# A two-layer encoder on one core: queries and splits moved a block ahead in attention, two PSUM banks kept across its borders, and four reorderings of sums and splits further on

## The chip, the cores and the metric

The kernel runs on one core of a Trainium2 chip. The metric is the device time of one execution in microseconds (us); before the change it is 1671.56, the median of three runs (1671.12 to 1671.75).

## What is computed

The reference is a trunk of two layers with shared weights over two requests, a prompt of 512 tokens and a sample of 256, D = 1024, all float32. The kernel treats both as one matrix of T = 768 tokens, kept transposed (features on partitions).

```python
for i in range(2):
    h = rms_norm(x, norm_mix[i])
    if i == 0:   # 16 heads of 64, 4 key/value groups, keys within 128 tokens, T5 bias, a sink logit per head
        x = x + window_attention(h, attn_w_qkv[0], attn_w_o[0], attn_sink[0], band_bias, in_window)
    else:        # (b_gate * conv3(c_gate * u)) @ w_out
        x = x + short_conv(h, conv_w_in[0], conv_w[0], conv_w_out[0])
    h = rms_norm(x, norm_mlp[i])
    x = x + jnp.square(jax.nn.relu(h @ mlp_w_up[i])) @ mlp_w_down[i]      # hidden size 4096
    gate = jax.nn.sigmoid(rms_norm(x, norm_ple[i]) @ ple_w_gate[i])
    x = x + (p[i] @ ple_w_proj[i]) * gate
return rms_norm(x, final_norm)
```

In attention a block of 128 queries meets the two or three key blocks around it; the softmax has the sink logit in its maximum and its sum.

## The kernel before

**Arithmetic.** A float32 product is made of three matmuls of a rounded type: every operand is split in a high part (a copy on ScalarE, ACT) and a low part (source minus high part, on VectorE, DVE), and high x high, high x low and low x high are added up in PSUM. Tile names carry it: whi and wlo, zhi and zlo, vhi and vlo are parts of a weight, xs those of an activation, aos those of an attention output. Weights come as raw tiles (wraw) by DMA from SyncE (SP). Some low parts are made without DVE: `added` (L453, L455) writes the negative high part on ACT and lets an accumulating DMA, issued by GpSimd (POOL), add the weight onto it.

**Stages.** First `mixer_attention`: norm, keys, values and queries of the first heads, then `attend(g)` for the four key/value groups, each over six query blocks n (four of the prompt, two of the sample). A block (g, n) makes for each of four heads a score tile S on TensorE (PE) (L716, L717), adds the bias and takes the maximum on DVE (L718), the exponential on ACT (L738), scales by the reciprocal sum (one head on ACT, L744, three on DVE, L746), transposes (pt, L751), splits the transposed weights in ph (ACT, L759) and pl (DVE, L760), and multiplies by the values (O, L761, L762). Then come the output projection (`first_head`, `first_tail`: L129), the MLP, the gated embedding (`ple`), the convolution mixer, its projection, the second MLP and the second gated embedding.

**Work beside attention.** The order of instructions in the attention stage is set by a scheduler from the dependences and the order in the code. Its PE would run dry while a block's softmax is under way, so the table `beside` puts other work behind certain blocks: `queries(c)` (the queries of two heads: product, split in qh and ql, and the DMAs of L633 that lay them out as q), `keys1`, `projected` (a projection of the per-layer embedding, whose results go out as pjs), `begin_output` (splits the heads of the first two groups into aos) and `first_output` (the first part of the output projection, whose sums go to xa, L785). Queries stand behind blocks (g, 2) and (g, 4), the projection behind (1, 5), the output's two steps behind (2, 5).

**PSUM.** There are eight banks. The attention stage uses one pool with S and product tiles until keys, values (vp, evicted to vv at L667) and first queries are done, then another (scores S 3 banks, products 2, O 1, pt 2); after attention all eight are in a third pool with the tags A, C and B (4, 2 and 2 banks). A new pool's tile waits for the release of the old pool's tiles in whose banks it lies. `fresh` hands out the tags in the cycle A, C, A, B; `shift` counts them.

**After attention** the order of PE, ACT and DVE is that of the code. The MLP and the convolution work on chunks of weights (`Weights7`): two raw tiles give seven products instead of eight, from four parts (w11 and w12, "direct"; w21 and w22, "second") and sums of them, s3 and s2 ("s32", made by `sums32`, L417 and L418, and split in zhi and zlo) and s1 and s4 ("s14", `sums14`, L422 and L423). `high`, `low` and `split` make the parts of such a group (L442 on ACT, L462 on DVE). `up_begun` and `up_first` begin the first MLP while the norm is still being computed; its plain chunk (L1183) uses "direct" through the tiles zhi and zlo and "second" through whi and wlo. `up_plain` follows, and then `up` for the remaining chunks, with the first of them treated apart (`first`). Each chunk prepares the next chunk's weights v between its own products; `late()` issues the activations that the previous chunk left over. Matmuls of one product carry tile names a, b, c and d (L484). In the convolution mixer `plain` (L1759) does the first chunk and `seven` the others.

Of the kernel before, what the change touches and what calls it, by code (L numbers as in the profile page):

```python
# [11 lines left out]
F32 = mybir.dt.float32  # L12
# [3 lines left out]
PSUM = bass.MemoryType.PSUM  # L16
DRAM = bass.MemoryType.DRAM

P = 128
D = 1024  # L20
KB = D // P
# [8 lines left out]

BM, BS, BO, BT, BL = 1, 3, 1, 2, 5

# [15 lines left out]
def trunk_kernel(ctx: ExitStack, tc: tile.TileContext, a: dict, out: bass.AP):  # L48
# [7 lines left out]
    stat = ctx.enter_context(tc.tile_pool(name="stat", bufs=1))  # L56
    dram = ctx.enter_context(tc.tile_pool(name="dram", bufs=1, space=DRAM))

    act.preload_act_table_set(EXP_LN)
    tmp, turn, shift = None, 0, 0  # L60

# [43 lines left out]
    def bank(tag, name):  # L105
        return psum.tile([P, 512], F32, tag=tag, name=name, bufs=BANKS[tag])

# [381 lines left out]
    def mixer_attention():  # L489
# [10 lines left out]
        def pair(j, name, dt=F32):  # L500
            return main.tile([P, 2, T], dt, tag=f"x{j}", name=name)
# [40 lines left out]
        with tc.manual_schedule(engines=order):  # L542
# [39 lines left out]

            bp = psum.tile([P, 512], F32, tag="S", name="bp", bufs=2)
            pe.matmul(bp[:HEADS, :], lhsT=rb[:], rhs=oh[:], start=True, stop=True)
# [6 lines left out]
        with s1:  # L591
# [46 lines left out]
            rc = ap.tile([P, T // P], F32, name="rc", bufs=1)  # L638
            rt = psum.tile([P, 512], F32, tag="S", name="rt", bufs=2)
            for n in range(T // P):  # L640
# [15 lines left out]
            def values(n):  # L656
                ps = psum.tile([P, 512], F32, tag="S", name="vp", bufs=2)
                for k in range(KB):
                    xh, xl = (xs[i][k][:, n * P : (n + 1) * P] for i in range(2))
                    wh, wl = wv[0][k], wv[1][k]  # L660
                    pe.matmul(ps[:, :256], lhsT=xh, rhs=wh, start=k == 0, stop=False)
                    pe.matmul(ps[:, :256], lhsT=xh, rhs=wl, start=False, stop=False)
                    pe.matmul(ps[:, :256], lhsT=xl, rhs=wh, start=False, stop=k == KB - 1)
                src = ps[:, :256].rearrange("p (g d) -> p g d", g=KV)
                hi, lo = vv[:, n, :, 0, :], vv[:, n, :, 1, :]
                act.activation(hi, src, AF.Copy, scale=rc[:, n : n + 1])
                dve.scalar_tensor_tensor(lo, src, rc[:, n : n + 1], hi.bitcast(F32), ALU.mult, ALU.subtract)  # L667
# [25 lines left out]
            bands(0)  # L693

            def attend(g):
                heads[g] = pair(g, "heads")
                if g < KV - 1:
# [3 lines left out]
                for s in SEQS:  # L701
                    hi_blk = lo_blk + s // P
                    for n in range(lo_blk, hi_blk):
# [6 lines left out]
                        for hp in range(2):  # L710
                            L = ap.tile([P, 2, 384], F32, tag="L", name="L", bufs=BL)
                            for j in range(2):
                                h = REP * g + 2 * hp + j
                                S = psum.tile([P, 512], F32, tag="S", name="S", bufs=BS)
                                q = qst[h][:, n * P : (n + 1) * P]
# [91 lines left out]

            def projected():
                w = weight(a["proj"][1, 0], 2)
                for m in range(KB // 2):  # L810
                    step(1, m, w, part1, "t", False)

# [10 lines left out]
            def begin_output():  # L823
# [166 lines left out]
    def first_tail(norm, places, output, product, ws):  # L990
# [10 lines left out]
        c = ws[1]  # L1001
        m6, m7 = KB - 1, KB // 2 - 1
        ps = [output(m) for m in (m6, m7)]
        pjs.extend(product(m) for m in range(KB // 2))
        add(m6, ps[0], xa[m6])
# [23 lines left out]
    def mlp(l, norm, nxt, w, places, early, product=None, begun=None):  # L1029
# [5 lines left out]
        groups = [{k: {} for k in QS7.values()} for _ in range(NG)]  # L1035
        pend = []

# [77 lines left out]
        def up_first(ps, w, v, parts, s1):  # L1115
# [30 lines left out]
            for i in range(2):  # L1146
                for o in range(2):
                    rectified(y[i], ps[i][o], H * o, H * o + H, ALU.max)
                if i == 0:
# [5 lines left out]
                    s3.high(1)  # L1155
                    s3.added(1)
            pend.extend(acts_of(0, *y, y[1]))
            return v

        def up_plain(u, w, make, then):  # L1160
# [15 lines left out]
            for n, (i, ks, sides) in enumerate(order):  # L1176
# [15 lines left out]
                elif begun and n == 1:  # L1192
# [3 lines left out]
                    steps[1]()  # L1196
                    steps[2]()
                    v.split("direct")
                    steps[3]()
# [50 lines left out]
        def up(u, w, make, then):  # L1250
# [181 lines left out]
    def ple(norm, nxt):  # L1432
# [38 lines left out]
        with tc.manual_schedule(engines={ET.Activation, ET.PE, ET.DVE}):  # L1471
# [187 lines left out]
    def mixer_conv(norm, w, v, norm_parts, held, finals, places, nxt):  # L1659
# [124 lines left out]
        def seven(kind, p, w, make, first, last):  # L1784
# [186 lines left out]
```

## Time and profile before

| | us |
|---|---|
| median of three runs | 1671.56 |
| profiled execution | 1671.81 |
| its span | 1669.8 |
| PE busy in it | 1641.9 |
| DVE busy | 1381.3 |
| ACT busy | 949.1 |
| POOL busy | 71.9 |

The profile is of one execution; all times inside it count from the start of its span, and its own time is 2.0 longer than the span. An idle time in brackets is what an engine stood still ahead of an instruction, with the instruction that let it go. L12 is line 12 of the kernel before. The matmuls' ends are modelled, so a matmul shows as busy a little past the start of the next one.

### The profile page before, as it was taken

The page shows a single profiled execution, that of the slowest core. Times are in us where ns is not written, and L with a number is a line of the kernel's source. Part 1 is how long each engine was busy: PE and PEld are TensorE (multiplying, and loading weights), DVE is VectorE, ACT ScalarE, POOL GpSimd, SP SyncE. Part 2 cuts the span into 40 slices and gives each one's busy share as a digit, 9 for nine tenths or more (in the row PEclk, how much of TensorE's full clock was granted, in tenths as well). Part 3 has the DMA queues.
Part 4 walks back from the last instruction along what each step waited for, and adds up shares of the span by engine and source line. Part 5 has one row for each costly group of instructions (what it writes and reads, how often), then busy time and mean ns, then how long its engine had stood idle before and what let it go on. Part 6 is the DMA issues. An engine that isn't in the chain of part 4 may idle for free.

```text
span 1669.8 us, 24311 instructions
## 1 busy us (share of the span) xinstructions
PE 1641.9 (98%) x9414; PEld 1588.0 (95%) x9414; DVE 1381.3 (83%) x2242; ACT 949.1 (57%) x1508; POOL 71.9 (4%) x104
## 2 busy tenths in 40 slices
PE   8999999999999999999999999999999999999997
PEld 7888788999999999999999999999999999999986
DVE  7499888789889889877888787868889988988676
ACT  7377756765555556554654334545556555655454
POOL 0211000010000000000000000000000000000000
PEclk9999999999999999999999999999999999999998
DMA  8755312433333322341312222122333223333132
GB/s 265 192 152 144 101 59 75 121 96 82 95 95 95 94 85 77 93 123 64 101 61 76 76 66 76 61 76 64 95 95 95 87 78 90 95 95 106 65 92 98
DMA packets 55476, 161.11 MB, mean 96 GB/s; under 512 B 7056, under 2 KB 10128, under 8 KB 55360
## 3 DMA queue, kind: packets, MB, share of 16 engines
q1 hardware_dynamic: 45184, 139.89, 26.2%
q0 software_dynamic: 10176, 19.67, 6.7%
q8 instruction: 74, 1.21, 0.3%
q14 instruction: 42, 0.34, 0.1%
HBM read 138.82 MB, written 10.48 MB: 89 GB/s over the span
## 4 chain that ended last, share of the span: by engine, by line
PE 84%; DVE 9%; ACT 4%; issue 2%; DMA 1%; SPq 0%; DVEq 0%; ACTq 0%
PE a L484 31%; PE mm L129 10%; PE mm L138 8%; PE b L484 8%; PE c L484 4%; PE d L484 4%; PE B L484 4%; PE C L484 4%; PE gate L138 3%; PE pt L751 1%; PE p L1080 1%; PE p L1183 1%; PE gate L129 1%; PE O L761 1%; PE S L716 1%
## 5 line engine op out<-in xcount | busy, mean ns | idle before, releaser
L484 PE MATMUL a<-xs,whi 128*128 128x384 f32 x624 | 121.7, 336 | 0.0
L442 ACT ACTIVATE vhi<-wraw 128x512 fp32r<-128x512 f32 x67 | 42.2, 630 | 132.3 <-PE B L484 87.9
L484 PEld LDWEIGHTS a<-xs,whi 128*128 128x128 f32 x624 | 110.1, 188 | 0.1
L484 PE MATMUL a<-t,zhi 128*128 128x384 f32 x536 | 109.1, 336 | 0.0
L484 PE MATMUL a<-t,whi 128*128 128x384 f32 x536 | 108.8, 336 | 0.0
L484 PE MATMUL b<-t,zhi 128*128 128x384 f32 x536 | 108.7, 336 | 0.0
L1329 DVE TENSOR_TENSOR x<-x,a 128x384 f32<-128x384 f32 x112 | 62.1, 554 | 55.2 <-PE a L484 55.2
L484 PE MATMUL a<-act,whi 128*128 128x384 f32 x448 | 96.6, 337 | 0.0
L484 PEld LDWEIGHTS a<-t,whi 128*128 128x128 f32 x536 | 94.9, 188 | 0.0
L484 PEld LDWEIGHTS b<-t,zhi 128*128 128x128 f32 x536 | 94.9, 188 | 0.0
L484 PEld LDWEIGHTS a<-t,zhi 128*128 128x128 f32 x536 | 94.8, 188 | 0.0
L462 DVE TENSOR_TENSOR wlo<-wraw,whi 128x1024 fp32r<-128x1024 f32 x70 | 85.3, 1219 | 7.6 <-ACT whi L442 7.6
L442 ACT ACTIVATE whi<-sum 128x1024 fp32r<-128x1024 f32 x67 | 70.6, 1054 | 27.1 <-PE a L484 22.7
L462 DVE TENSOR_TENSOR wlo<-sum,whi 128x1024 fp32r<-128x1024 f32 x67 | 81.8, 1221 | 5.0 <-ACT whi L442 5.0
L1042 ACT ACTIVATE y<-y 128x768 f32<-128x768 f32 x64 | 53.7, 839 | 56.0 <-DVE y L1039 55.9
L138 PE MATMUL mm<-xs_mix,whi 128*128 128x512 f32 (+1 forms) x320 | 83.1, 342 | 0.0
L462 DVE TENSOR_TENSOR zlo<-sum,zhi 128x1024 fp32r<-128x1024 f32 x67 | 81.6, 1217 | 0.0
L484 PEld LDWEIGHTS a<-act,whi 128*128 128x128 f32 x448 | 79.8, 188 | 0.0
L442 ACT ACTIVATE whi<-wraw 128x1024 fp32r<-128x1024 f32 x72 | 75.7, 1051 | 6.8 <-PE C L484 6.8
L442 ACT ACTIVATE zhi<-sum 128x1024 fp32r<-128x1024 f32 x67 | 70.9, 1058 | 10.8 <-DVE sum L418 9.9
L484 PE MATMUL a<-xs,wlo 128*128 128x384 f32 x312 | 67.1, 336 | 0.0
L83 ACT ACTIVATE whi<-wraw 128x1024 fp32r<-128x1024 f32 (+2 forms) x49 | 49.9, 1019 | 29.5 <-PE mm L129 9.7
(345 smaller groups left out, 4555.4 us busy)
## 6 DMA issues: line engine op xcount, KB each, us to landing
wraw<-in_up SPq DMA_DIRECT2D x64, 512.0 KB, 3.7
wraw<-in_down SPq DMA_DIRECT2D x64, 512.0 KB, 4.2
wraw<-in_w_in SPq DMA_DIRECT2D x24, 512.0 KB, 3.5
wraw<-in_gate SPq DMA_DIRECT2D x16, 512.0 KB, 3.5
vlo<-in_up POOLq DMA_DIRECT2D x28, 256.0 KB, 5.5
vlo<-in_down POOLq DMA_DIRECT2D x28, 256.0 KB, 5.8
pj<-pjs SPq DMA_DIRECT2D x16, 384.0 KB, 2.9
wraw<-in_w_q SPq DMA_DIRECT2D x8, 512.0 KB, 4.6
```

The source lines that it names most:

```text
L83: first = act.activation(hi, src, AF.Copy)
L129: pe.matmul(t, lhsT=w, rhs=x[:, o:e], start=first and i == 0 and j == 0, stop=last and i == n - 1 and j == 2)
L138: pe.matmul(ps[:, o:e], lhsT=w, rhs=x[:, o:e], start=i == 0 and j == 0, stop=i == n - 1 and j == 2,)
L442: act.activation(hi[:], src, AF.Copy)
L462: dve.tensor_tensor(lo[:], src, hi[:].bitcast(F32), ALU.subtract)
L484: pe.matmul(ps, lhsT=a, rhs=b, start=start and i == 0, stop=i == len(terms) - 1, skip_group_check=True)
L716: pe.matmul(S[:, :w], lhsT=q, rhs=khh[g][:, k0 * P : k0 * P + w], start=True, stop=False)
L751: pe.transpose(pt[:, h * P : (h + 1) * P], lg[h // 2][:, h % 2, b * P : (b + 1) * P], ident[:],)
L761: pe.matmul(O[:], lhsT=v, rhs=ph[:], start=b == 0, stop=False)
L1042: act.activation(t[:], t[:], AF.Square)
L1080: pe.matmul(ps[o], lhsT=wt[:, c], rhs=xs[f"x{h + 1}{1 + o}"][m][part], start=k == 0 and j == 0, stop=k == KB - 1 and j == 2,)
L1329: dve.tensor_tensor(t[:, o : o + H], t[:, o : o + H], f, op)
```

## The change

No product is added or left out. Six things are moved.

1. A pool `pair_of_banks` with two PSUM banks lives for the whole kernel, and tag B always comes from it; the small products bp and rt, the values' product vp and two of three score tiles S use it too. The third score tile has one bank of the stage's pool. `shift` begins at 2 and is lowered by two in `first_tail`, so that the first output product lies in B and the tags further on stay mostly as they were.
2. In attention, queries go behind blocks (g, 1) and (g, 3), the projection is halved over (1, 4) and (1, 5), and `begin_output` goes behind (2, 4).
3. In the first MLP's beginning, the "direct" weight is split ahead of the "second" one and of the activations' low parts, and one `added` of an activation moves into the next chunk.
4. In both MLPs the first `up` chunk gets the order of the others.
5. At the border to the convolution, `sums32` moves behind the residual's last block.
6. In three of the convolution's chunks the low part of "s32" is made ahead of the product's last step `top`.

```diff
+    pair_of_banks = ctx.enter_context(tc.tile_pool(name="psB", bufs=2, space=PSUM))
-    tmp, turn, shift = None, 0, 0
+    tmp, turn, shift = None, 0, 2
...
     def bank(tag, name):
-        return psum.tile([P, 512], F32, tag=tag, name=name, bufs=BANKS[tag])
+        pool = pair_of_banks if tag == "B" else psum
+        return pool.tile([P, 512], F32, tag=tag, name=name, bufs=BANKS[tag])
...
-                ps = psum.tile([P, 512], F32, tag="S", name="vp", bufs=2)
+                ps = bank("B", "vp")
...
+            def third():
+                return psum.tile([P, 512], F32, tag="S", name="S", bufs=1)
...
-                                S = psum.tile([P, 512], F32, tag="S", name="S", bufs=BS)
+                                S = third() if scores % 3 == 1 else bank("B", "S")
+                                scores += 1
...
             beside = {
                 (0, 5): (inputs1, keys1),
-                (1, 5): (projected,),
-                (2, 5): (begin_output, first_output),
+                (1, 4): (lambda: projected(0),),
+                (1, 5): (lambda: projected(1),),
+                (2, 4): (begin_output,),
+                (2, 5): (first_output,),
             }
...
-                    beside[g, 2 + 2 * n] = (lambda c=2 * g + 2 + n: queries(c),)
+                    beside[g, 1 + 2 * n] = (lambda c=2 * g + 2 + n: queries(c),)
...
         ps = [output(m) for m in (m6, m7)]
+        shift -= 2
...
-            v.added("second")
+            v.high("direct")
             s1.low(0)
             s1.low(1)
-            v.high("direct")
             s2.t13()
             s2.high(0)
             v.low("direct")
+            v.added("second")
...
                     s3.high(1)
-                    s3.added(1)
             pend.extend(acts_of(0, *y, y[1]))
+            aside.append(lambda: s3.added(1))
...
             if seven:
-                if not first:
-                    v.sums14()
+                v.sums14()
                 v.high("s32")
-            if not first:
-                late()
+            late()
...
-            if first:
-                late()
-                if seven:
-                    v.sums14()
             late()
...
-            v.sums32()
             added()
             nxt.plain_block(m, x(m))
+            v.sums32()
...
             product7(a, w, "s4", xs, False)
+            if busy and not last:
+                v.low("s32")
             top(kind, p, a, H)
```

On DVE at the entry to `attend`, around the last value tile's eviction (vv) and the first scores' reductions (L718, which is L727 after), before:

```order
L84 TENSOR_TENSOR ql<-qt,qh 128x768
L667 SCALAR_TENSOR_TENSOR vv<-vp,rc,vv 128x4x64
L718 ISA L,mx<-S,bias,sink 128x256
L718 ISA mx 128x1
L718 ISA L,mx<-S,bias,sink 128x256
```

The same place after:

```order
L85 TENSOR_TENSOR ql<-qt,qh 128x768
L727 ISA L,mx<-S,bias,sink 128x256
L727 ISA mx 128x1
L669 SCALAR_TENSOR_TENSOR vv<-vp,rc,vv 128x4x64
L727 ISA L,mx<-S,bias,sink 128x256
```

The first score's reduction has passed the last eviction.

On DVE where the head tiles are split (aos), between block (2, 5)'s reductions and its scales, before (nm, es and sm are a block's maxima and sums):

```order
L718 ISA L,mx<-S,bias,sink 128x256
L718 ISA mx 128x1
L84 TENSOR_TENSOR aos<-heads,aos 128x768
L769 TENSOR_TENSOR heads<-O,ot 64x2x128 x2
L731 TENSOR_SCALAR nm<-mx 128x4
L733 TENSOR_TENSOR es<-sink,mx 128x4
L84 TENSOR_TENSOR aos<-heads,aos 128x768 x3
L739 TENSOR_TENSOR sm<-sm,es 128x4
```

After, a block earlier, the first split stands among the scales of a block (L755), and further down three stand together:

```order
L749 RECIPROCAL sm<-sm 128x4
L85 TENSOR_TENSOR aos<-heads,aos 128x768
L755 TENSOR_SCALAR L<-L,sm 128x256
L769 TENSOR_TENSOR pl<-pt,ph 128x512
L755 TENSOR_SCALAR L<-L,sm 128x256 x2
```

```order
L778 TENSOR_TENSOR heads<-O,ot 64x2x128 x2
L740 TENSOR_SCALAR nm<-mx 128x4
L742 TENSOR_TENSOR es<-sink,mx 128x4
L85 TENSOR_TENSOR aos<-heads,aos 128x768 x3
L748 TENSOR_TENSOR sm<-sm,es 128x4
```

One split has moved ahead; the three others still stand in a row ahead of the next block's sums.

On ACT at the beginning of the first MLP (q and t are steps of the activations' splits), before:

```order
L327 ACTIVATE q<-x,vec 128x768 x2
L442 ACTIVATE whi<-wraw 128x1024
L453 ACTIVATE wlo<-whi 128x1024
L442 ACTIVATE zhi<-wraw 128x1024
L356 ACTIVATE t_3865<-q 128x768
```

The same place after:

```order
L329 ACTIVATE q<-x,vec 128x768 x2
L444 ACTIVATE zhi<-wraw 128x1024
L358 ACTIVATE t_3863<-q 128x768
L444 ACTIVATE whi<-wraw 128x1024
L455 ACTIVATE wlo<-whi 128x1024
```

zhi has passed whi and wlo, and one t has passed them too.

More of the change, by code (lines that the diff above doesn't have):

```diff
@@ L29 @@
 CH = 1024
-BM, BS, BO, BT, BL = 1, 3, 1, 2, 5
+BM, BO, BT, BL = 1, 1, 2, 5
 NA = 1
@@ L581, in mixer_attention @@
                     wq = [fetch(a["w_q"][0])]
-            bp = psum.tile([P, 512], F32, tag="S", name="bp", bufs=2)
+            bp = bank("B", "bp")
             pe.matmul(bp[:HEADS, :], lhsT=rb[:], rhs=oh[:], start=True, stop=True)
@@ L638, in mixer_attention @@
             rc = ap.tile([P, T // P], F32, name="rc", bufs=1)
-            rt = psum.tile([P, 512], F32, tag="S", name="rt", bufs=2)
+            rt = bank("B", "rt")
             for n in range(T // P):
@@ L693, in mixer_attention @@
             bands(0)
+            scores = 0
+            def third():
+                return psum.tile([P, 512], F32, tag="S", name="S", bufs=1)
             def attend(g):
+                nonlocal scores
                 heads[g] = pair(g, "heads")
@@ L806, in keys1, with projected @@
                 keys(1, products(terms_of(weight(a["w_k"][1], KB), xs)))
[L808 to L811, printed above, removed]
+            projw = []
+            def projected(n):
+                if n == 0:
+                    projw.append(weight(a["proj"][1, 0], 2))
+                for m in range(2 * n, 2 * n + 2):
+                    step(1, m, projw[0], part1, "t", False)
             part1 = [], []
@@ L1002, in first_tail @@
         m6, m7 = KB - 1, KB // 2 - 1
+        nonlocal shift
         ps = [output(m) for m in (m6, m7)]
+        shift -= 2
         pjs.extend(product(m) for m in range(KB // 2))
@@ L1035, in mlp @@
         groups = [{k: {} for k in QS7.values()} for _ in range(NG)]
-        pend = []
+        pend, aside = [], []
         def rectified(t, src, o, e, op):
@@ L1197, in up_plain @@
                     steps[2]()
+                    for step in aside:
+                        step()
                     v.split("direct")
```

## Prediction

> **What bounds the kernel now.** I read the profile's page first: the share of each engine, then the chain that ended last.
>
> ```profile
> span 1669.8 us, 24311 instructions
> PE 1641.9 (98%) x9414; PEld 1588.0 (95%) x9414; DVE 1381.3 (83%) x2242; ACT 949.1 (57%) x1508; POOL 71.9 (4%) x104
> ...
> PE 84%; DVE 9%; ACT 4%; issue 2%; DMA 1%; SPq 0%; DVEq 0%; ACTq 0%
> ```
>
> TensorE (PE) is busy for 98% of the span and owns 84% of the chain. The change neither adds nor removes a matmul, so nothing can be gained but PE's waits. Which they are stands in the table of waits on PE (line, tile waited for, its producer: us in total, times, longest).
>
> ```profile
> PE mm L138 <- ACT p0h L83: 6.0, 1, 6.0
> PE b L484 <- DVE zlo L462: 1.4, 2, 0.7
> ...
> PE S L716 <- DMA q<-ql: 1.3, 2, 0.9
> PE S L716 <- DVE vv L667: 1.1, 1, 1.1
> PE mm L129 <- ACT whi L83: 1.0, 1, 1.0
> ...
> PE mm L138 <- DVE aos L84: 0.8, 1, 0.8
> PE a L484 <- DVE wlo L462: 0.8, 2, 0.4
> PE pt L751 <- ACT L L744: 0.7, 3, 0.3
> PE c L1759 <- ACT xs L310: 0.7, 1, 0.7
> PE p L1183 <- DVE zlo L462: 0.6, 1, 0.6
> PE c L1759 <- DVE xs L311: 0.4, 1, 0.4
> PE O L762 <- DVE pl L760: 0.4, 1, 0.4
> PE p L1183 <- ACT zhi L442: 0.2, 1, 0.2
> ```
>
> The first row is the program's start, which the change leaves alone. The other twelve lie at places that it touches: 17 waits, 9.4 us printed. The printed idle falls short of the delay, because a matmul counts as busy past the moment at which the next could have started. Three rows of the timeline, from one of the width-3 convolution's chunks, show by how much.
>
> ```profile
> 909.29 1.38 PE L484 MATMUL b<-t,zhi 128*128 128x384 f32 x7
> 910.78 0.96 PE L484 MATMUL b<-t,zlo 128*128 128x384 f32 x4
> ...
> 909.51 1.22 DVE L462 TENSOR_TENSOR zlo<-sum,zhi 128x1024 fp32r<-128x1024 f32 x1
> ```
>
> Four matmuls take 0.96, seven 1.38, so starts lie 0.14 to 0.17 apart (0.17 in an undisturbed stream) while one lasts some 0.34. The eighth was due at 909.29 + 7 x 0.17 = 910.50 and came at 910.78, just behind zlo (909.51 + 1.22 = 910.73): a delay of 0.27 without any idle in the table. A printed idle is therefore about 0.17 short. The 17 waits are worth 9.4 + 17 x 0.17 = 12.3 us, and that, with what the next parts add, is the ceiling.
>
> **Entry to attention.** The value product's last eviction (line 667) holds the first score.
>
> ```profile
> 72.00 0.48 DVE L667 SCALAR_TENSOR_TENSOR vv<-vp,rc,vv 128x256 fp32r<-128x256 f32 x1 [1.18 <-ACT vv L666]
> ...
> 72.54 0.39 PE L716 MATMUL S<-khh,q 128*128 128x256 f32 x1 [1.08 <-DVE vv L667]
> ```
>
> S starts 0.06 behind that eviction's end, 72.48, because the scores' pool took over the banks of the closed one. With two banks kept, the first S needs the bank of the value tile but one, and VectorE (DVE) now has the first score's reduction ahead of the last vv. The delay, 1.08 + 0.17 less what remains in the second score, gives **-1.1** (-0.9 to -1.2).
>
> **End of attention.** The table blames ScalarE (ACT) for the output projection's wait; the timeline has two DVE and PE rows that say otherwise.
>
> ```profile
> 274.08 0.41 DVE L785 TENSOR_TENSOR xa<-xa,mm 128x256 f32<-128x256 f32 x1
> ...
> 274.59 0.94 PE L129 MATMUL mm<-aos,zhi 128*128 128x384 f32 x4 [1.00 <-ACT whi L83]
> ```
>
> The product reads zhi, not whi. It starts 0.10 behind the end of the last xa, 274.49: again new banks over old ones. On a kept B bank it needs nothing that is late. PE was free at 274.59 - 1.17 = 273.42, the first product is 12 matmuls x 0.17 = 2.1 us, so the second, on the old banks, is due at 275.5, a us past 274.49. **-1.0** (-0.9 to -1.1).
>
> **Queries a block sooner, the projection split.** The two DMA waits and one full softmax delay read thus on PE:
>
> ```profile
> 160.67 0.36 PE L716 MATMUL S<-khh,q 128*128 128x256 f32 x1 [0.48 <-DMA q<-ql]
> ...
> 162.00 0.36 PE L716 MATMUL S<-khh,q 128*128 128x256 f32 x1 [0.85 <-DMA q<-ql]
> ...
> 170.22 0.34 PE L717 MATMUL S<-kll,q 128*128 128x384 f32 x1
> ...
> 178.38 1.09 PE L751 MATMUL pt<-ident,L 128*128 128x128 f32 x8 [0.27 <-ACT L L744]
> ```
>
> The q transfers are issued a block earlier, so both waits go: 1.33 + 0.34 = 1.7. The three pt waits (0.7 + 0.5 = 1.2) belong to the order that is dissolved. What takes their place is shorter cover: the last two rows give 178.38 - 170.56 = 7.8 us from a block's last score to its first transpose, under load, all of it covered but 0.27. Counting the new order's matmuls at the trace's spacings, my estimate of the products behind the last score is 4.8 us in block (1,5), 6.6 in (2,2) and 4.6 in (2,4); the other blocks behind which something moves keep over 8. A new wait can so cost nothing (the chain was shorter than 7.8 where DVE was free) up to 7.8 - 4.8 = 3.0. Walking DVE and ACT through the new order with the trace's durations, I get 1.2 and take that: -1.7 - 1.2 + 1.2 = **-1.7** (-2.9 to +0.2). SP carries the same loads, the q copies one block earlier; POOL's order is unchanged.
>
> **begin_output a block sooner.** Its four splits of the head tiles (aos) cost DVE 0.9 us each, and PE waited for the first, then ran at half clock (two rows of PE, one of DVE, and two windows: PE, PEld, DVE, ACT, POOL, granted clock, DMA).
>
> ```profile
> 204.16 0.50 PE L762 MATMUL O<-pl,vv 128*128 128x512 f32 x1 [0.43 <-DVE pl L760]
> ...
> 206.84 0.79 PE L138 MATMUL mm<-aos,whi 128*128 128x512 f32 x1 [0.77 <-DVE aos L84]
> ...
> 205.83 0.95 DVE L84 TENSOR_TENSOR aos<-heads,aos 128x768 fp32r<-128x768 f32 x1
> ...
> 207.00:208.00 1.00, 1.00 (x3) 0.81 (x4) 0.95 (x5) 0.19 (x1) 0.00 (x0) 0.50 1.05 230
> ...
> 209.00:210.00 1.00, 1.00 (x5) 0.90 (x5) 1.00 (x2) 0.99 (x5) 0.00 (x0) 0.50 1.03 378
> ```
>
> The delays here are 0.8 + 0.17 for aos and 0.4 + 0.17 for pl, and three us at clock 0.50 lose 1.5: 3.0 in all. In the new order one split is early, but three (2.9 us) still stand together ahead of the next block's scale. I estimate a wait of about 1.7 for them and the halved clock again, against 3.0 before; with further small waits the walk comes out even: **0** (-3 if all goes, +2 if the three splits are waited for in full).
>
> [...]
>
> **First MLP's border.** ACT makes the second weight's high and low parts ahead of the direct weight's zhi.
>
> ```profile
> 322.92 1.04 ACT L442 ACTIVATE whi<-wraw 128x1024 fp32r<-128x1024 f32 x1
> ...
> 324.96 1.04 ACT L442 ACTIVATE zhi<-wraw 128x1024 fp32r<-128x1024 f32 x1
> ...
> 326.04 1.23 DVE L462 TENSOR_TENSOR zlo<-wraw,zhi 128x1024 fp32r<-128x1024 f32 x1 [2.00 <-ACT zhi L442]
> ```
>
> With zhi at 322.92 and zlo right behind, both waits go (0.2 + 0.6 + 2 x 0.17 = 1.2): **-1.2** (-1.3 to -0.6, if the norm's pieces crowd zlo). The price is wlo of "second", which POOL's DMA completes and which now starts two us later, behind zhi and a t. The POOL issue, the landing times of line 455, and PE's first use:
>
> ```profile
> 325.54 0.90 POOL L455 DMA_DIRECT2D wlo<-in_up  x1 [20.16 <-PE p L1080]
> ...
> DMA to landing us min/median/max: 4.0/4.8/5.6
> ...
> 335.77 0.34 PE L1183 MATMUL p<-x,wlo 128*128 128x384 f32 x1
> ```
>
> 327.6 + 5.6 = 333.2 against 335.8 - 1.2 = 334.6: a margin of 1.4, so nothing is paid.
>
> **First `up` chunk in the common order.** Twice, PE waits for wlo (0.4) and zlo (0.7): 1.1 + 0.34 = 1.4 per MLP. In the second MLP DVE idles just ahead of the late work:
>
> ```profile
> 1152.16 0.56 DVE L1290 TENSOR_TENSOR y<-a,p 128x384 f32<-128x384 f32 x1 [1.50 <-PE a L484]
> ```
>
> The sums s14 move into that hole of 1.5, and zlo comes so much sooner: **-1.4** (-0.7 to -1.5). In the first MLP DVE has no such hole; only the earlier border helps, by about 2 on DVE and 1.2 on PE. I take **-1.0** (0 to -1.4).
>
> **Convolution border.** DVE adds two halves of the s32 sum ahead of the residual that xs is made from.
>
> ```profile
> 862.06 0.68 DVE L417 TENSOR_TENSOR sum<-wraw 128x512 f32<-128x512 f32 x1
> ```
>
> Moving both halves back brings x and then xs 1.3 us sooner, and the two c waits (0.7 + 0.4 + 0.34 = 1.4) go. DVE has the same work ahead of the norm's sum of squares, so part comes back there: half is taken, **-0.8** (-0.4 to -1.5). **seven:** zlo, ahead of `top`, no longer ends behind its first use: three chunks x 0.27, some kept, **-0.6** (0 to -0.8).
>
> **The sum.** -1.1 - 1.0 - 1.7 + 0 - 1.2 - 1.4 - 1.0 - 0.8 - 0.6 = -8.8. The profiled execution took 1671.81 (2.0 around its span), 0.25 above the median of 1671.56. Off the median: 1662.8, said as **1663**. The low ends add to -14.6 (1657), the high ends to -1.4 (1670).
>
> **Rivals.**
>
> *The softmax chain becomes the bound.* At (1,5), (2,2) and (2,4) the cover is 3.0, 1.2 and 3.2 us short of the 7.8 seen: 7.4 if the chain stays as long. Three halvings of the clock add 4.5, and the three splits cost their +2. Against -1.7 - 1.2 and the other parts' -7.1 that is +3.9: 1675.5. For it: DVE is at 83%, and 7.8 was just covered. Against it: with less queued behind the scores the chain is shorter too. It decides once these places wait for over 10 us together. Chance 0.06.
>
> *The clock is not halved* after the splits: 1.5 less, 1661.3. Chance 0.25. The three us at 0.50 speak against it; that one split is early and a wait may be spread out speaks for it. [...]
>
> *The gains come back at the next late step:* banks 2.0, second MLP 0.7, border 0.6, convolution 0.4, the rest nothing: -3.7, with +0.2 at the queries 1668. For it: DVE is near full at each place, so a step moved ahead makes another late. Chance 0.19, half of it beyond the bound below.
>
> *wlo lands late:* the chain slips 2 us more than reckoned and the margin of 1.4 is overdrawn by 0.6 + 0.17: 1663.6. Chance 0.05.
>
> **How the numbers follow.** The forecast has 0.45. A measurement here tells about 0.2% (3.3 us) from no change, so faster means below 1668.2. The forecast, the unhalved clock, late wlo and half of the third rival give 0.85; the other half and a third of the softmax rival give 0.11; 0.04 is slower. The range runs from the low ends' 1657 to 1669, short of the high ends by one because they would all have to fall together.
>
> **What would show it.** Right: no vv wait at the first S and no whi wait at the first output product; no q DMA wait near 160; no zlo wait in the first MLP; in the second MLP no b wait; the c waits gone, a small ss wait in their place; PE still at 0.50 for about 3 us near 205. Wrong: pt or O waits over 2 us together between 145 and 200, more slices at 0.50, or wlo waits near 334.

## The result, and the profile after

The changed kernel takes 1662.35 us, the median of six runs (1659.25 to 1662.74), against 1671.45 for the kernel before in the same session: a ratio of 0.9942, with a 95% interval of 0.9929 to 0.9955. The forecast was 1663. The profiled execution took 1661.51 with a span of 1659.5, that is 10.3 less than the span before.

The page's first lines and the table of waits on PE, after (the changed kernel's line numbers run two to sixteen ahead; columns as before):

```profile
span 1659.5 us, 24297 instructions
PE 1637.6 (99%) x9414; PEld 1587.3 (96%) x9414; DVE 1380.8 (83%) x2242; ACT 948.5 (57%) x1508; POOL 71.7 (4%) x104
```

```profile
PE mm L140 <- ACT p0h L84: 6.1, 1, 6.1
PE mm L140 <- DVE aos L85: 1.6, 1, 1.6
...
PE pt L760 <- ACT L L753: 0.6, 1, 0.6
PE ss L238 <- DVE al L85: 0.5, 1, 0.5
PE O L770 <- DVE heads L778: 0.4, 1, 0.4
PE b L486 <- DVE zlo L464: 0.4, 1, 0.4
PE c L1771 <- DVE xs L313: 0.3, 1, 0.3
PE O L771 <- DVE pl L769: 0.2, 1, 0.2
```

Of the twelve rows named in the prediction, those for vv, whi, q and wlo and ACT's for xs are gone, as are both waits of L1199 (L1183 before). The wait for aos is twice as long; one for heads and one for al are new. The sign "no zlo wait in the first MLP" came only in part: the 0.4 for b is in the first MLP's first `up` chunk.

Where the time went can be told to a few hundredths, because PE runs the same matmuls in both kernels. The timeline's PE rows give the starts of seven of them: the first score (S), the first output product (mm<-aos,zhi), the first b<-t,zhi of the first MLP, the first c<-xs,zhi of the convolution, the first a<-xs,whi behind it, the first mm<-ys,whi, and the final norm's first ss<-acc_final. The first column of the table runs from the span's start, the others from one of these starts to the next.

| us | to first S | to output product | to b | to c | to a | to ys | to final norm |
|---|---|---|---|---|---|---|---|
| before | 72.54 | 202.05 | 71.28 | 512.34 | 19.43 | 162.53 | 615.87 |
| after | 70.89 | 198.90 | 69.56 | 511.45 | 18.74 | 161.43 | 614.28 |
| difference | -1.65 | -3.15 | -1.72 | -0.89 | -0.69 | -1.10 | -1.59 |
| predicted | -1.1 | -2.7 | -1.2 | -1.0 | -0.8 | -0.6 | -1.4 |

Behind the final norm's start the profile after is 0.5 longer. The sum is -10.3 in this pair of profiles, -9.1 between the medians. Of the first column's 1.65 only 1.25 is the change's: from the first value product to the first score it is 18.49 us before and 17.24 after. The rest lies in the program's start, which differs from one profile to the next (see "The clock" below).

The rows that answer to those shown of before, PE and DVE at the two borders of attention: no idle ahead of the first score, the last vv behind the first score's reduction, none ahead of the output product.

```profile
70.89 0.28 PE L725 MATMUL S<-khh,q 128*128 128x256 f32 x1
...
269.79 0.85 PE L131 MATMUL mm<-aos,zhi 128*128 128x384 f32 x4
```

```profile
71.33 0.48 DVE L727 CUSTOM_DVE_ANT_0 L<-S,bias,sink 128x256 f32<-128x256 f32 x1 [0.91 <-PE S L726]
...
71.74 0.48 DVE L669 SCALAR_TENSOR_TENSOR vv<-vp,rc,vv 128x256 fp32r<-128x256 f32 x1
```

Where the aos splits lie, PE's row, DVE's row with three splits, and two windows (granted clock is the third number from the end):

```profile
202.48 0.79 PE L140 MATMUL mm<-aos,whi 128*128 128x512 f32 x1 [1.56 <-DVE aos L85]
...
201.47 2.69 DVE L85 TENSOR_TENSOR aos<-heads,aos 128x768 fp32r<-128x768 f32 x3
```

```profile
203.00:204.00 1.00, 1.00 (x4) 0.73 (x3) 1.00 (x2) 0.70 (x4) 0.00 (x0) 0.50 0.55 218
204.00:205.00 1.00, 1.00 (x5) 0.90 (x4) 1.00 (x6) 0.18 (x1) 0.00 (x0) 0.50 0.00 0
```

And in the first MLP zlo is ready before its first use, while the POOL issue of wlo starts 1.87 behind PE's first zhi product instead of ahead of it, and lands late:

```profile
320.54 0.51 PE L1199 MATMUL p<-x,zhi 128*128 128x384 f32 x2
320.89 0.34 PE L1199 MATMUL p<-x,zlo 128*128 128x384 f32 x1
...
329.25 0.34 PE L1199 MATMUL p<-x,wlo 128*128 128x384 f32 x1
...
322.41 0.90 POOL L457 DMA_DIRECT2D wlo<-in_up  x1 [22.07 <-ACT wlo L455]
```

```profile
DMA to landing us min/median/max: 6.5/6.5/6.5
```

### The profile page after: what moved, and what is told of

Read it like the earlier page. It is cut to its first block, busy times and chain, and to the rows that moved or that the text cites. A ratio compares the mean times of both kernels' runs of the same rounds, so it can differ in the third digit from the quotient of the medians.

```text
span 1659.5 us, 24297 instructions
## 1 busy us (share of the span) xinstructions
PE 1637.6 (99%) x9414; PEld 1587.3 (96%) x9414; DVE 1380.8 (83%) x2242; ACT 948.5 (57%) x1508; POOL 71.7 (4%) x104
## 4 chain that ended last, share of the span: by engine, by line
PE 88%; DVE 7%; ACT 4%; issue 1%; DMA 0%; DVEq 0%; SPq 0%; ACTq 0%
PE a L486 33%; PE mm L131 10%; PE mm L140 8%; PE b L486 8%; PE d L486 5%; PE c L486 5%; PE B L486 4%; PE C L486 4%; PE gate L140 3%; PE pt L760 1%; PE p L1096 1%; PE p L1199 1%; PE gate L131 1%; PE O L770 1%; PE O L771 1%
## 5 line engine op out<-in xcount | busy, mean ns | idle before, releaser
L358 ACT ACTIVATE t<-y 128x768 fp32r<-128x768 f32 x56 | 45.7, 838 | 34.9 <-DVE y L349 34.4
```

The lines of the kernel that those rows point to most:

```text
L358: act.activation(t[0][:], (self.q1, self.q2)[i][:], AF.Copy)
```

## The experiments

**Theory:** each part pays for the waits at its own place, and the parts add up. **Rivals:** the gain belongs to the attention stage as a whole; the later reorderings only move a wait to the next late step. Each part was undone in the changed kernel or done alone, then three kernels went after the waits that remain.

The stretches of every kernel, defined as above (the last two columns of the table above are given only where they differ from 161.43 and 614.28 by over 0.1):

| us | to first S | to output product | to b | to c | to a | later | median |
|---|---|---|---|---|---|---|---|
| banks undone | 72.57 | 199.02 | 69.90 | 511.35 | 18.73 | | 1662.70 |
| table undone | 70.53 | 208.29 | 69.56 | 511.47 | 18.74 | | 1670.28 |
| begin_output back | 71.25 | 200.14 | 69.56 | 511.50 | 18.72 | | 1663.11 |
| banks alone, on before | 70.99 | 208.52 | 71.06 | 512.42 | 19.42 | 162.53, 615.86 | 1675.29 |
| border undone | 71.24 | 199.00 | 71.06 | 512.33 | 18.72 | | 1663.78 |
| first chunk undone | 71.09 | 197.55 | 69.56 | 512.35 | 18.73 | 615.86 | 1662.01 |
| convolution undone | 69.77 | 197.58 | 69.56 | 511.47 | 19.45 | | 1663.06 |
| seven undone | 70.28 | 197.62 | 69.61 | 511.47 | 18.75 | 162.54 | 1660.89 |
| splits sooner | 70.59 | 197.79 | 69.56 | 511.44 | 18.72 | | 1660.02 |
| splits on GpSimd | 71.36 | 201.50 | 69.56 | 511.45 | 18.73 | | 1663.65 |
| zlo sooner in up | 70.61 | 197.65 | 69.56 | 511.44 | 18.77 | | 1659.79 |
| cover moved | 70.32 | 197.88 | 69.56 | 511.51 | 18.75 | | 1660.22 |

A stretch that an edit does not touch repeats to within 0.1 us behind the output product. The medians do not: they carry 1 us or more that has nothing to do with the edit, for a reason that the first two columns show below.

**1. The banks undone.** Tag B, the small products, vp and the scores come from the stages' own pools again.

```diff
-        pool = pair_of_banks if tag == "B" else psum
-        return pool.tile([P, 512], F32, tag=tag, name=name, bufs=BANKS[tag])
+        return psum.tile([P, 512], F32, tag=tag, name=name, bufs=BANKS[tag])
...
-                                S = third() if scores % 3 == 1 else bank("B", "S")
+                                S = psum.tile([P, 512], F32, tag="S", name="S", bufs=3)
```

> The changed kernel (1662.35 us) with the kept pair of banks taken back, all else changed. Theory (each part pays for the waits at its own place): the first score waits about 1.1 us for the last vv again and the first output product about 1.0 us for the last xa, so 1664.4 us. Rival (the attention stage as a whole sets the gain; the banks only shift waits to the next late step): within 0.5 us of 1662.35, with no vv wait over 0.3 us.

The ratio to before is 0.9941 (0.9929 to 0.9954): by the median the rival looks right. The table of waits says otherwise:

```profile
PE mm L129 <- ACT whi L83: 1.2, 1, 1.2
PE S L723 <- DVE vv L667: 1.1, 1, 1.1
```

Both waits are back near the predicted size, and from the first value product to the first score it takes 18.49 us again. What hid them in the median seems to be the clock: in this profile the 1.6 wait for aos was not followed by half clock (1.00 in each window from 196 to 208), in the changed kernel's it was (0.50 from 203 to 205). The runs point the same way: their mean granted clock is 0.998 in four of five here, and 0.996 in four of the changed kernel's six.

**2. The banks alone, on the kernel before.**

> The kernel before (1671.45 us) with the kept pair of banks as the only change. Theory: the vv wait at the first score and the wait at the first output product go, and nothing else moves: 1671.45 - 2.1 = 1669.4 us. Rival (a shift of the schedule undoes it): within 0.5 us of 1671.45.

Theory and rival are both wrong: 1675.29 against 1671.4, a ratio of 1.0018 (1.0009 to 1.0027), slower. The two border waits went, yet attention became 6.5 us longer. From its table of waits:

```profile
PE S L725 <- DMA q<-ql: 4.1, 3, 2.1
PE mm L140 <- DVE aos L85: 2.8, 1, 2.8
...
PE pt L760 <- ACT L L753: 0.9, 1, 0.9
```

The order of attention is the scheduler's, and with the banks it came out differently: a score that needs q stands close behind q's copy, and the landing shows. The landings of q between 90 and 170 us, with the banks alone, in the kernel before and in the changed kernel:

```profile
DMA to landing us min/median/max: 2.7/4.8/7.7
```

```profile
DMA to landing us min/median/max: 3.1/4.9/7.3
```

```profile
DMA to landing us min/median/max: 2.7/3.5/4.4
```

So the median landing is no longer than in the kernel before (4.8 against 4.9), but the scores are nearer to them: at the longest q wait (2.1, at 117.80) the copies are issued from 109.33 on, against 107.65 before, and the row of scores begins at 115.04, against 117.02. Why the wait for aos grew from 0.8 to 2.8 was not followed.

Half clock follows twice, once behind a q wait and once behind aos (one PE row and one window of each):

```profile
163.98 0.36 PE L725 MATMUL S<-khh,q 128*128 128x256 f32 x1 [1.74 <-DMA q<-ql]
...
213.19 0.80 PE L140 MATMUL mm<-aos,whi 128*128 128x512 f32 x1 [2.76 <-DVE aos L85]
```

```profile
166.00:167.00 1.00, 1.00 (x6) 0.80 (x5) 0.38 (x2) 0.00 (x0) 0.00 (x0) 0.50 0.96 381
...
217.00:218.00 1.00, 1.00 (x4) 0.81 (x4) 0.14 (x1) 0.00 (x0) 0.00 (x0) 0.50 0.83 197
```

It lasts 10.2 us in all, against 3.4 in the kernel before. Half of the added 6.8, less PE's idle time in it, makes my estimate that about 3 of the 6.5 us are the clock's.

**3. The table undone.**

```diff
-                (1, 4): (lambda: projected(0),),
-                (1, 5): (lambda: projected(1),),
-                (2, 4): (begin_output,),
-                (2, 5): (first_output,),
+                (1, 5): (lambda: projected(0), lambda: projected(1)),
+                (2, 5): (begin_output, first_output),
...
-                    beside[g, 1 + 2 * n] = (lambda c=2 * g + 2 + n: queries(c),)
+                    beside[g, 2 + 2 * n] = (lambda c=2 * g + 2 + n: queries(c),)
```

> The changed kernel with the table of work beside attention as before (queries behind (g,2) and (g,4), projection whole behind (1,5), begin_output behind (2,5)). Theory: the two waits for q's DMA and the three small pt waits come back, the 0.8 us wait of pt at 159 goes: about 1664.0 us. Rival (the table gains nothing, because the shorter cover takes back what the earlier queries give): within 0.5 us of 1662.35. In both the aos wait is about 0.8 us again instead of 1.6, and TensorE still runs at half clock for about 3 us behind it.

1670.28, ratio 0.9986 (0.9977 to 0.9995): the table is worth 9.4 us of attention with the banks in place, over five times what either theory or prediction gave it. The waits are those of the banks alone (q 4.2, aos 2.8), and half clock lasts 10.3 us, which by the same estimate is about 3 of the 9.4. Experiments 1 to 3 and the kernel before make a square for the attention stretch: neither 202.05, banks only 208.52, table only 199.02, both 198.90. So the parts do not add up here. The banks cost 6.5 with the old table. With the new one, under which no profile shows a wait for q, they gain: 199.02 was measured at full clock and 198.90 was not, and the changed kernel's attention at full clock takes 197.6 (experiments 6 to 8), so that the banks are worth 1.4 there, the wait at the output product.

**4. begin_output back, alone.**

```diff
-                (2, 4): (begin_output,),
-                (2, 5): (first_output,),
+                (2, 5): (begin_output, first_output),
```

> The changed kernel with begin_output alone put back behind (2,5). Theory (prediction: this step comes out even, 0 within -3 to +2): the aos wait falls from 1.6 to about 0.8 us, the halved clock stays, a pl wait of 0.4 us comes back: within 0.8 us of 1662.35. Rival (a block sooner is where the gain of the attention stage comes from): 1664 us or more.

1663.11, ratio 0.9944 (0.9932 to 0.9956). By the median, 0.8 above the changed kernel's, the theory's time holds; its mechanism does not. The attention stretch is 1.24 longer than in the changed kernel, with half clock in both. The aos wait did not fall to 0.8 but went, and one of equal kind came up: the next block's score waited for a reduction that ended on DVE at 202.52, ahead of the splits (from 203.65).

```profile
202.57 0.39 PE L725 MATMUL S<-khh,q 128*128 128x256 f32 x1 [1.09 <-DVE mx L727]
```

So by the stretch a block sooner gains 1.2, neither the zero expected nor the rival's 1.7 and more.

**5. The first MLP's border undone.**

```diff
-            v.high("direct")
+            v.added("second")
             s1.low(0)
             s1.low(1)
+            v.high("direct")
             s2.t13()
             s2.high(0)
             v.low("direct")
-            v.added("second")
```

The edit also puts `s3.added(1)` back.

> The changed kernel with the old order at the first MLP's beginning (second weight and activations' lows ahead of the direct split). Theory: the two waits for zhi and zlo come back, 1.2 us, and up to 0.9 us in the first up chunk behind it: 1663.6 to 1664.5 us. Rival (ScalarE and VectorE are near full here, so the order only moves the wait): within 0.5 us of 1662.35.

1663.78, ratio 0.9952 (0.994 to 0.9965). The stretch to b gives back 1.50, that to c 0.88: 2.4 in all, a little over the theory's upper end of 2.1. The second part shows as a wait of the first `up` chunk, PE's row there:

```profile
352.70 1.67 PE L486 MATMUL a<-xs,whi 128*128 128x384 f32 x8 [0.73 <-DVE y L1306]
```

With DVE's chain late, the common order makes the chunk's second half wait for y, which stands behind the sums s14 (L1306 is L1290 of before).

**6. The first `up` chunk undone, in both MLPs.**

```diff
             if seven:
-                v.sums14()
+                if not first:
+                    v.sums14()
                 v.high("s32")
-            late()
+            if not first:
+                late()
...
             rectified(y1, c, 0, H, ALU.max)
+            if first:
+                late()
+                if seven:
+                    v.sums14()
             late()
```

> The changed kernel with the first up chunk in its old order in both MLPs. Theory: in the second MLP waits of 0.4 and 0.7 us come back (1.4 us of delay); in the first MLP, where VectorE has no idle stretch, at most 0.5 us: 1663.8 to 1664.3 us. Rival (the first MLP's gain came from this reorder and not from the earlier border): the first MLP shows waits of 0.4 and 0.7 us as before, and the total is 1664.6 us.

The table of waits has 1.4 for b<-zlo and 0.7 for a<-wlo again, 0.9 of delay in the first MLP (511.45 to 512.35) and 1.58 in the second. As the rival said, the first MLP has both its waits again; that the gain there is this reorder's alone does not hold, as experiment 5 shows. The median, 1662.01, ratio 0.9948 (0.9935 to 0.996), shows none of these 2.5 us: its attention stretch is 1.35 shorter than the changed kernel's, without a change there. Its windows at the place show why:

```profile
202.84 0.50 PE L140 MATMUL mm<-aos,whi 128*128 128x512 f32 x1 [1.55 <-DVE aos L85]
```

```profile
203.00:204.00 1.00, 1.00 (x6) 0.87 (x7) 1.00 (x2) 1.00 (x5) 0.00 (x0) 1.00 0.88 353
204.00:205.00 1.00, 1.00 (x7) 0.87 (x6) 1.00 (x5) 0.07 (x1) 0.00 (x0) 1.00 0.02 6
```

The same wait, 1.55 against 1.56, and the clock stays at 1.00. What is left of the 2.5 shows between the profiled executions, 1662.49 against 1661.51.

**7. The convolution's border undone.**

```diff
+            v.sums32()
             added()
             nxt.plain_block(m, x(m))
-            v.sums32()
```

> The changed kernel with the s32 sums ahead of the residual again at the convolution's border. Theory: the c waits become 0.7 and 0.4 us (1.5 us of delay against 0.4 now), the wait of ss for al falls from 0.5 us to nothing: 0.6 us slower, 1663.0 us. Rival (what is saved at c all comes back at ss): within 0.2 us, with the same place's sum of waits unchanged.

The stretch gives back 0.71, of a possible 1.4: theory. c waits 0.8 and 0.4 again and the wait for al is gone. Of the 1.10 that the move saves ahead of ss, 0.41 come back there. The median, 1663.06, ratio 0.9947 (0.9934 to 0.9961), agrees by luck: the five runs lie at 1660.1 to 1660.5 and at 1663.1 to 1663.3, and the profiled one of 1660.09 is the shortest.

**8. seven undone.**

```diff
-            if busy and not last:
-                v.low("s32")
```

> The changed kernel without the earlier low part of s32 in the convolution's three chunks. Theory: three delays of 0.27 us come back, 0.8 us, with no idle in the table of waits: 1663.2 us. Rival (those delays belong to the matmul stream itself): no change, and the eighth matmul of each b product still starts 0.17 us behind the seventh.

The stretch to ys gives back 1.11, more than the theory's 0.8, though the median, 1660.89 (ratio 0.9941, 0.9928 to 0.9953), is below the changed kernel's. PE's rows of the first of the three chunks show the delay without a bracket; after it, in the changed kernel, there is none:

```profile
899.36 1.38 PE L486 MATMUL b<-t,zhi 128*128 128x384 f32 x7
900.85 0.96 PE L486 MATMUL b<-t,zlo 128*128 128x384 f32 x4
901.65 1.56 PE L486 MATMUL a<-t,zhi 128*128 128x384 f32 x8
```

```profile
901.01 1.56 PE L486 MATMUL b<-t,zhi 128*128 128x384 f32 x8
902.41 0.86 PE L486 MATMUL b<-t,zlo 128*128 128x384 f32 x4
```

The first row begins with the second of eight products. 900.85 - 899.36 - 7 x 0.175 = 0.27 against 902.41 - 901.01 - 8 x 0.175 = 0. Behind the delay come 0.10 more: the four products with zlo take 901.65 - 900.85 = 0.80 to the next product's start, and 0.70 in the changed kernel (four times 0.175). Three chunks with 0.37 each are the 1.11.

**9. The splits sooner.** Group 0 behind (2,3), group 1 behind (2,4).

```diff
-                (2, 4): (begin_output,),
+                (2, 4): (lambda: split_heads(1),),
...
+            beside[2, 3] += (lambda: split_heads(0),)
```

> The changed kernel with the head splits of group 0 behind block (2,3) and those of group 1 behind (2,4), instead of both behind (2,4). Theory (three splits in a row on VectorE are what the first output product waits for, and that wait halves the clock): with at least one more split early the wait falls from 1.6 to 0.7 us or less; without a wait over 0.4 us there are no slices at 0.50: 1660 to 1661.5 us. Rival (the tiles come free only when the last queries are done, so the split waits and blocks VectorE): no gain or up to 2 us slower, with new waits of pt or S between 180 and 195 us.

1660.02, ratio 0.9935 (0.9923 to 0.9948). aos waits twice 0.4, and the clock stays at 1.00. But a wait of 0.9 for a reduction (mx) joins them, so that the stretch, 197.79, is no shorter than in kernels with the one long wait and full clock (197.55 to 197.65). Its gain is that of the clock. The time is the theory's and there are no slices at 0.50, as it said; but the mx wait is 0.94 and the clock stayed at 1.00, so a wait over 0.4 did not bring half clock here, and one profile at full clock could be luck, since five of seven kernels with the long wait had it too. The rival's new wait is there, at 202.05 and not between 180 and 195.

**10. The early splits on GpSimd.**

```diff
-                    split(hi[:], lo[:], heads[g][:, i, :])
+                    if g < 2:
+                        act.activation(hi[:], heads[g][:, i, :], AF.Copy)
+                        nc.gpsimd.tensor_tensor(lo[:], heads[g][:, i, :], hi[:].bitcast(F32), ALU.subtract)
+                    else:
+                        split(hi[:], lo[:], heads[g][:, i, :])
```

> The changed kernel with the low parts of the four early head tiles made on GpSimd instead of VectorE. Theory: VectorE loses 3.6 us of work between 193 and 204 us; if GpSimd takes about twice VectorE's 0.9 us for one, four in a row still end later than now and the first output product waits 2 us or more, with the half clock: 1662 to 1665 us. Rival (VectorE's queue is what matters, since three splits stand ahead of softmax steps): the wait falls below 1 us: 1660 to 1661 us.

1663.65, ratio 0.9955 (0.9941 to 0.9968): the theory's time, not its mechanism. aos waits only 0.6, as the rival said, but three scales on DVE took 5.58. DVE and POOL rows of the place:

```profile
193.91 5.58 DVE L755 TENSOR_SCALAR L<-L,sm 128x256 f32<-128x256 f32 x3
...
193.86 5.48 POOL L788 TENSOR_TENSOR aos<-heads,aos 128x768 fp32r<-128x768 f32 x3 [28.55 <-ACT aos L787]
```

Three scales that take 0.88 together elsewhere (before, L746, at 195.76) lasted 5.58 beside POOL's three splits (5.48), and pt waited 0.81 and 1.48 for them. Half clock followed from 199.1 to 205.9, 6.8 against 3.4 in the changed kernel; the stretch of 201.50 has both in it.

**11. zlo sooner in the up chunks.**

```diff
             product7(a, w, "s4", xs, False)
+            if seven:
+                v.low("s32")
             rectified(y1, a, H, T, ALU.max)
```

> The changed kernel with the same move made in the MLP's up chunks: the low part of s32 ahead of the last rectification of the chunk before. Theory: the one wait for zlo left in the first MLP (0.4 us idle, 0.54 us of delay) goes, and nothing else waits: 1661.8 us. Rival (the rectified y1 is then late for the next chunk's down products): waits for act or xs of the MLP of over 0.3 us, no gain.

The zlo wait went, and the stretch is 511.44 against 511.45: no gain. PE now stands ahead of a<-t,zhi (355.25, where 354.94 was due), for the copy of that chunk's c on ACT. So the rival's "no gain" holds, by another wait than the one it named. The median, 1659.79 (ratio 0.9936, 0.9923 to 0.9948), is 2 us below the 1661.8 expected, for another reason: its attention stretch was at full clock.

**12. The cover moved,** on top of 9.

```diff
-                for m in range(2 * n, 2 * n + 2):
+                for m in ((0,), (1, 2, 3))[n]:
```

> The kernel of the sooner head splits (1660.02 us) with the projection divided one to three over blocks (1,4) and (1,5) instead of two to two. Counted from the order of the instructions, the cover behind the last score of block (1,5) grows from 4.8 to 7.3 us and that of (2,2) from 6.6 to 9.2. Theory (the cover is what decides whether the transposes wait): the pt wait of 0.6 us near 159 falls below 0.1, the stage from the first score to the first output product is 0.8 us shorter than in the run with the sooner splits alone, 197.0 us, and the median is 1659.2 us. Rival (VectorE and ScalarE are what is late there, whatever stands behind the score): the wait stays at 0.4 us or more, and no gain.

1660.22, ratio 0.9935 (0.9921 to 0.9948). The pt wait near 159 went, as the cover said. In its place stand two others, PE's rows:

```profile
154.83 0.39 PE L725 MATMUL S<-khh,q 128*128 128x256 f32 x1 [0.29 <-DVE mx L727]
...
156.13 0.74 PE L140 MATMUL mm<-p,whi 128*128 128x512 f32 x2 [0.39 <-ACT pjs L541]
```

The stretch is 197.88, so both theory's mechanism and rival's "no gain" hold. The intervals of 9, 11 and 12 overlap with the changed kernel's; none of them is shown to be better than it.

## Why the prediction was right, and where its steps were not

**Borders of attention.** -1.1 and -1.0 were the waits' sizes, and experiment 1 brings them back at 1.1 and 1.2 printed, worth 1.25 and 1.4 in the stretches. What the prediction did not ask is whether the banks leave the rest of the stage alone. Without the table they do not (experiment 2: +6.5). That nothing else moved held only because the two edits came together.

**The size of a wait.** The prediction put a printed idle 0.17 short of the delay. Its own rows show 0.10 more: the four products with zlo behind the wait last 0.96, and 0.86 where nothing waits. So these waits cost 0.27 more than is printed, and most terms came out larger than forecast: seven 1.11 for 3 x 0.27, the second MLP 1.58 for 1.4, the first MLP's border 1.50 for 1.2.

**Queries and projection.** The q waits went and one pt wait of 0.6 came up near 159, as walked through (1.2 taken, about 0.9 of delay found: 0.62 + 0.27). The waits of pt and O between 145 and 200 come to 1.2, under the 2 that were to speak for the softmax rival. The term of -1.7 is what the table gains over before; given the banks it gains 9.4. The change's largest single effect is thus no gain over before but the repair of a loss that the other edit brings.

**begin_output.** Predicted even, with a wait of 1.7 and half clock; the profile after has 1.56 and half clock. Experiment 4 puts the step at -1.2: mis-sized, since the alternative under the new table was worse than the old row showed.

**First MLP.** The border was -1.2, and 1.50 came back on undoing it: the waits' 0.23 + 0.64 printed and 2 x 0.27, and 0.1 that no row shows. The first chunk's -1.0 was -0.89, but the step that gave it failed: it said that in this MLP only the earlier border helps and the reorder does little. Undoing the border costs 0.88 there and undoing the reorder 0.90: each alone is worth nothing, both together 0.9. Without the border DVE's chain is late and the new order waits for y; without the new order zlo is late whatever the border does. The price of the later wlo was nothing, as said, but the margin was not 1.4: issue 322.41 + 6.5 = 328.9 against the first use at 329.25 leaves 0.3. The landing term of 5.6 was mis-sized, and the rival of a late wlo was close.

**Second MLP, convolution, seven.** -1.4 was -1.59, -0.8 was -0.69 with the wait for al in its place, both by the stated mechanism. seven's -0.6 was -1.10, outside its range: the three delays went whole, and each was 0.37 and not 0.27.

**The clock.** Half clock came, as forecast, in the profile after. But it is no fixed price. Seven profiles have the same wait for aos of 1.5 to 1.6: the clock fell with it in two (after, border undone) and stayed in five, and the attention stretch differs accordingly, 198.90 and 199.00 against 197.55 to 197.65 (experiment 1's 199.02 has the output product's delay of 1.20 + 0.27 in it, 197.55 without). The rival without half clock and the forecast are thus two outcomes of one kernel, 1.3 us apart.

How long it lasted is read from the windows. Two of the changed kernel's:

```profile
202.00:203.00 1.00, 0.52 (x1) 0.50 (x2) 1.00 (x2) 1.00 (x6) 0.00 (x0) 0.62 1.05 399
...
205.00:206.00 1.00, 1.00 (x5) 0.80 (x5) 1.00 (x6) 0.33 (x1) 0.00 (x0) 0.67 0.00 0
```

A mean of 0.62 is 0.76 us at half clock, so the clock falls at 202.24; in the same way it rises at 205.66, 3.42 later. Read so, half clock in attention lasted 3.40 to 3.42 us in the kernel before (from 206.88), in experiments 4 and 5 (from 203.50 and 203.18) and in the first stretch of experiments 2 and 3 (from 164.74 and 164.08), and 6.82 to 6.84 in their second (from 212.52 and 211.86) and in experiment 10 (from 199.12). Ahead of 206.88 PE had waited 0.43 and 0.77, the rows in the prediction. In the changed kernel it waited 1.56 and the clock fell; in experiment 6 it waited 1.55 and the clock stayed at 1.00. So the size of the wait alone does not tell whether the clock falls, and what does was not shown.

The start differs from profile to profile too, while the granted clock reads 1.00: the first products begin two in 0.64 us or more, and later two in 0.35, in the changed kernel from 11.27 on. The windows of experiment 7's profile have 4 matmuls in the us from 8 and 7 in that from 9, those of experiment 10's have 3 in the us from 10 and 6 in that from 11, and the first score comes at 69.77 and 71.36. By my estimate start and aos wait together can move one kernel by some 3 us (1.6 + 1.3). Its six runs spread over 3.5, and the kernel before over 3.8 in another session (21 runs, 1670.64 to 1674.42). That the median came within 0.7 us of the forecast is therefore in part luck; the stretches before the final norm gained 10.8 against 8.8 forecast.

## What to carry to other kernels

Two edits can each be worth nothing or less and together pay: cost an edit in the company of the others, above all where a scheduler sets the order and a freed resource lets it choose anew. Compare kernels whose instructions are the same on the bound engine by the stretches between named instructions, which repeat to 0.1 us, before trusting medians that differ by 1 or 2 us, and see in both profiles where half clock began and ended. And a wait without a bracket is read from the spacing of starts.

## What the runs showed of the hardware

In experiment 10, while POOL subtracted three 128x768 tiles (1.85 us each by the mean of four, against 0.95 on DVE), three DVE scales of 128x256 took 5.58 us, and 0.88 in the kernel before: DVE's row ends at 199.49 and POOL's at 199.34. An accumulating DMA of one weight (512 KB) took 5.6 us to land before and 6.5 after, at the same place in the program. And in attention half clock lasted 3.40 to 3.42 us in six stretches and 6.82 to 6.84 in three.
